# First feed-forward block without Strassen pairs, and the down projection's first inputs in tiles of their own

## Chip, cores and metric

One core of a Trainium2 chip. The metric is the device time of one execution in microseconds (us). Matrix products run on TensorE; VectorE, ScalarE and GpSimd work beside it; SyncE's queue (SP) issues nearly all loads from HBM.

## What is computed

A decoder layer for 256 tokens of width 2048: a mixer with four branches, then a SwiGLU feed-forward part of width 5632, then a last RMSNorm. The change touches the feed-forward part and its two borders:

```python
h = h + mixed @ w_out
v = rms_norm(h, norm_ffn)
h = h + (silu(v @ w_ffn_gate) * (v @ w_ffn_up)) @ w_ffn_down
return rms_norm(h, norm_final)
```

All is float32. Each float32 product is made from three products of a faster format: an operand is split into a high part (ScalarE copies it, rounding) and a low part (VectorE subtracts), and high x high, high x low and low x high are added up in PSUM (`mm3`, `mm3s`).

## The kernel before, in words

**Common way.** The rows of a weight matrix are taken two k-tiles of 128 at a time, here called a k-pair. `wpiece` (lines 117 to 127) loads 256 x 512 weights (512 KB) into a `raw` tile on SP's queue, ScalarE makes `whi`, VectorE makes `wlo`; there are four slots of each. Per piece and block of 128 tokens there are six matmuls of 128 x 512.

**Strassen pairs.** `pair` (lines 243 to 292) multiplies the two token blocks with two column blocks of weights (`wl`, `wr`) at once. A k-pair in `skps` is made by Strassen's scheme with 7 products in place of 8, so 21 matmuls in place of 24. `s_weights` loads both pieces into one `sx` tile (1 MB, two slots), VectorE forms sums (`se`, `sx`) and all are split into `sh`, `sl`, `seh`, `sel`. The activations need four sums too: `s_sums` forms them in a scratch tile and splits them into `vsh`, `vsl`, which have three slots of four 128 x 128 blocks. `pair` adds up in eight PSUM banks named 1 to 8: a Strassen pair writes 1, 5, 7, 6 first and then 2, 3, 4; an ordinary k-pair writes 2, 3, 4, 8. When the last Strassen pair is done, `mid` is called: `mid_sums` combines banks 1, 5, 6, 7 into four tiles `u` (tags `u0` to `u3`). With no Strassen pair, `mid` is called at k-pair 2.

**Gate and up.** Eleven blocks `f` of 512 hidden columns, eight k-pairs each. Blocks 1 to 10 take k-pairs 0, 3 and 5 by Strassen, block 0 takes 0 and 3. After a block, `hd` (two token blocks x 512) is formed from the banks, the `u` tiles, Silu and a scale. `hid_out` is put off (`later`) to the `mid` of the next block: TensorE transposes `hd` (`trans_bank`, two banks), ScalarE copies into a tile `hs`, and GpSimd's queue stores `hs` to DRAM (`hid`, 512 KB) in one transfer.

**Down.** Two halves `cc` of the output columns, 22 k-pairs each, of which 0, 3, 6, 9, 12 go by Strassen. `h_of` loads a k-pair's hidden block from DRAM into `hv` (tags `u1` and `u3` by turns, 256 KB, SP's queue), splits it into one of four slots of `ah` and, for Strassen, forms the sums. `mid` adds the four `u` tiles into `hn`.

**Where things lie.** `sx`, `sh`, `se` and their like are in a pool opened after the mixer's pools are closed, so in the room of the mixer's tiles (`mth` among them). `vth` and `vtl`, the normalised input of gate and up, are in the pool `uv` under tags `th` and `tl`; `gfin` and `ah` of the down part take the same tags.

**Order.** The program is written in Python order; a planner reorders it by a simulated timeline and places all waits. Each engine and each queue then runs in the order given. Only a few instructions are pinned.

Of the kernel before, what the change touches and what calls it, by code (L numbers as in the profile page):

```python
# [8 lines left out]
F32 = mybir.dt.float32  # L9
F32R = mybir.dt.float32r  # L10
AF = mybir.ActivationFunctionType
ALU = mybir.AluOpType
AX = mybir.AxisListType

P = 128
S = 256
D = 2048
NKT = D // P
DFF = 5632
NFT = DFF // P  # L20
# [9 lines left out]
def hybrid_block_kernel(  # L30
# [7 lines left out]
    nc = tc.nc  # L38
# [5 lines left out]
    w_fg = w_ffn_gate[0]  # L44
    w_fu = w_ffn_up[0]
    w_fd = w_ffn_down[0]
# [9 lines left out]
    def act(o, i, f=AF.Copy, **kw):  # L56
        return nc.scalar.activation(o, i, f, **kw)  # L57

    def tt(o, a, b, op, eng=None):
        return (eng or nc.vector).tensor_tensor(out=o, in0=a, in1=b, op=op)  # L60
# [6 lines left out]
    def stt(o, a, s, b, op0, op1, **kw):  # L67
        return nc.vector.scalar_tensor_tensor(out=o, in0=a, scalar=s, in1=b, op0=op0, op1=op1, **kw)

    late = {"psum": None, "turn": 0}  # L70
# [7 lines left out]
    def rd(t):  # L78
        return t.bitcast(F32)
# [116 lines left out]

    def s_sums(v, sh, sl):

        w = late["tmp"].tile([P, 512], F32, tag="u0", name="ssum").rearrange("p (a b) -> p a b", a=4)
        a11, a21, a12, a22 = v[:, 0, 0:P], v[:, 0, P:S], v[:, 1, 0:P], v[:, 1, P:S]
        tt(w[:, 0, :], a21, a22, ALU.subtract)
        tt(w[:, 1, :], w[:, 0, :], a11, ALU.subtract)
        tt(w[:, 2, :], a11, a21, ALU.subtract)
        tt(w[:, 3, :], a12, w[:, 1, :], ALU.add)
        act(sh, w)
        tt(sl, w, rd(sh), ALU.subtract)
# [28 lines left out]
    def pair(wl, wr, nkp, skps, a_of, sx, mid, split=0):  # L237


        pq = late["psum"]  # L240
        names = (1, 5, 7, 6, 2, 3, 4, 8) if skps else (2, 3, 4, 8)
        b = {i: pq.tile([P, 512], F32, tag=f"p{i}", name=f"p{i}") for i in names}
        left = {2: nkp * 2 - len(skps), 3: nkp * 2 - len(skps), 4: nkp * 2 - len(skps), 8: 2 * (nkp - len(skps))}
        for i in (1, 5, 6, 7):
            left[i] = len(skps)
        begun = set()

        def go(i, a, w, pin=False):
            left[i] -= 1
            mm3s(b[i], a, w, i not in begun, left[i] == 0, pin)  # L250
            begun.add(i)

        held = []
        for kp in range(nkp):
            blk, sums = a_of(kp, kp in skps)
            if kp in skps:
                l1, l2, r2, t1, t2, t3, t4 = s_weights(wl, wr, kp, sx)
                go(1, blk(0, 0), l1)
                go(5, sums(0), t1)
                go(7, sums(2), t3)  # L260
                go(6, sums(1), t2)
                go(2, blk(1, 0), l2)
                go(3, sums(3), r2)
                go(4, blk(1, 1), t4)
                if kp == skps[-1]:
                    mid(b)
                continue
            if not skps and kp == 2:
                mid(b)
            rows = slice(kp * 2 * P, (kp + 1) * 2 * P)  # L270
            lh, ll = wpiece(wl[rows, :], 2, 512)
            rh, rl = wpiece(wr[rows, :], 2, 512)
            todo = [(i, [(blk(j, t), (wh[:, j, :], wl_[:, j, :])) for j in range(2)])
                    for i, t, wh, wl_ in ((2, 0, lh, ll), (3, 0, rh, rl), (4, 1, lh, ll), (8, 1, rh, rl))]
            if kp >= nkp - split:
                held.append(todo)
                continue
            for i, prods in todo:
                for a, w in prods:
                    go(i, a, w)  # L280
        for q in range(4):
            for todo in held:
                i, prods = todo[q]
                for a, w in prods:
                    go(i, a, w, pin=True)
        return b
# [503 lines left out]

    def hid_out(hd, f):

        hs = fp.tile([P, 4, S], F32, tag="hs", name="hs")
        for i in (0, 2):
            pt = trans_bank(hd, i, 2)
            act(hs[:, i:i + 2, :].rearrange("p a b -> p (a b)"), pt)
        d = dr.tile([P, 4, S], F32, name=f"hid{f}")
        nc.gpsimd.dma_start(d, hs)
        hid.append(d)

    def v_of(kp, with_sums):
        def blk(j, t):
# [8 lines left out]
    def mid_sums(b):  # L811

        u = [fp.tile([P, 512], F32, tag=f"u{i}", name="u") for i in range(4)]
        act(u[0], b[1])
        tt(u[2], u[0], b[6], ALU.add)
        tt(u[1], u[2], b[7], ALU.add)
        tt(u[2], b[5], u[2], ALU.subtract)
        tt(u[3], b[5], u[1], ALU.subtract)
        return u
# [5 lines left out]
    for f in range(DFF // 512):  # L825
        fs = slice(f * 512, (f + 1) * 512)
        kept = []

        def mid(b):
            kept.extend(mid_sums(b))  # L830
            run_later()

        b = pair(w_fg[:, fs], w_fu[:, fs], NKT // 2, FS[:2] if f == 0 else FS, v_of, sx, mid, split=1)
        hd = fp.tile([P, 2, 512], F32, tag="hd", name="hd")
        for t in range(2):
            tt(hd[:, t, :], kept[t], b[(2, 4)[t]], ALU.add)
            act(hd[:, t, :], hd[:, t, :], AF.Silu, scale=rstd2[:, t:t + 1])
            tt(kept[2 + t], kept[2 + t], b[(3, 8)[t]], ALU.add)
            stt(hd[:, t, :], kept[2 + t], rstd2[:, t:t + 1], hd[:, t, :], ALU.mult, ALU.mult)
        later.append(lambda hd=hd, f=f: hid_out(hd, f))  # L840


    gfin = uv.tile([P, D], F32, tag="th", name="gfin")
    nc.gpsimd.dma_start(gfin, norm_final.partition_broadcast(P))
    ss3 = small.tile([P, 2, 4], F32, name="ss3", bufs=1)
    pre3 = small.tile([P, 2], F32, name="pre3", bufs=1)
    ah = uv.tile([P, 4, 2, 2 * S], F32R, tag="tl", name="ah")
    DS = (0, 3, 6, 9, 12)

    def h_of(kp, with_sums):  # L850
        v = fp.tile([P, 512], F32, tag=("u1", "u3")[kp % 2], name="hv").rearrange("p (a b) -> p a b", a=2)
        nc.sync.dma_start(v, hid[kp // 2][:, kp % 2 * 2:kp % 2 * 2 + 2, :])
        q = kp % 4
        act(ah[:, q, 0, :], v.rearrange("p a b -> p (a b)"))
        tt(ah[:, q, 1, :], v.rearrange("p a b -> p (a b)"), rd(ah[:, q, 0, :]), ALU.subtract)
        if with_sums:
            i = DS.index(kp) % len(FS)
            s_sums(v, hsh[:, i], hsl[:, i])

        def blk(j, t):  # L860
            o = slice(j * S + t * P, j * S + (t + 1) * P)
            return ah[:, q, 0, o], ah[:, q, 1, o]
        return blk, lambda n: (hsh[:, i, n, :], hsl[:, i, n, :])

    hsh, hsl = vsh, vsl
    for cc in range(2):
        cols = [slice((2 * cc + i) * 512, (2 * cc + i + 1) * 512) for i in range(2)]

        def mid(b):
            u = mid_sums(b)  # L870
            for t in range(2):
                for i in range(2):
                    o = hn[:, t, cols[i]]
                    tt(o, o, u[2 * i + t], ALU.add)
            run_later()

        b = pair(w_fd[:, cols[0]], w_fd[:, cols[1]], NFT // 2, DS, h_of, sx, mid, split=2 if cc else 1)
        for t in range(2):
            for i in range(2):
                o = hn[:, t, cols[i]]  # L880
                tt(o, o, b[((2, 3), (4, 8))[t][i]], ALU.add)
                sumsq(ss3[:, t, 2 * cc + i:2 * cc + i + 1], o)
                if cc == 0 or i == 0:
                    tt(o, o, gfin[:, cols[i]], ALU.mult, nc.gpsimd)
            if cc == 0:
                continue
            ms3, r, z, r3, p3 = (small.tile([P, 1], F32, tag=f"r3{i}", name="r3") for i in range(5))
            nc.vector.tensor_reduce(out=p3, in_=ss3[:, t, 0:3], axis=AX.X, op=ALU.add)
            ts(p3, p3, 1.0 / D, EPS, ALU.mult, ALU.add)
            stt(ms3, ss3[:, t, 3:4], 1.0 / D, p3, ALU.mult, ALU.add)  # L890
            tt(r, ms3, mhalf[:, 0:1], ALU.pow, nc.gpsimd)
            tc.keep_in_program_order(tt(o, o, gfin[:, cols[1]], ALU.mult))
            stt(z, ms3, r, r, ALU.mult, ALU.mult)
            ts(z, z, -0.5, 1.5, ALU.mult, ALU.add)
            tt(r3, r, z, ALU.mult)
            for i in range(4):
                o = hn[:, t, i * 512:(i + 1) * 512]
                if i % 2:
                    act(o, o, scale=r3)
                else:  # L900
                    ts(o, o, r, z, ALU.mult, ALU.mult)
                nc.sync.dma_start(out[t * P:(t + 1) * P, i * 512:(i + 1) * 512], o)
# [31 lines left out]
```

## Time and profile before

| | us |
|---|---|
| median of 3 runs | 1555.77 (1554.59 to 1556.63) |
| the profiled execution | 1554.03 |
| its span | 1552.3 |

| engine | busy us | share of the span |
|---|---|---|
| TensorE, matmuls | 1506.3 | 97% |
| TensorE, weight loads | 1243.3 | 80% |
| VectorE | 1088.4 | 70% |
| ScalarE | 794.3 | 51% |
| GpSimd | 102.0 | 7% |

Mean granted TensorE clock of the span: 0.987 of full speed. The gate/up blocks run from 803 to 1279 us of the span, the down part from there to 1542.

How to read the rows: times are microseconds from the start of the span. A matmul's record lasts longer than the distance to the next one, as they are pipelined; a record is about 0.39 us. "[4.87 <-ACT ah L57]" says that the engine was idle for 4.87 us before this instruction, and that the wait was ended by ScalarE's write of `ah` in line 57. Lines 57, 60, 65 and 68 are helpers for one operation of ScalarE or VectorE each; tiles tell them apart. PE is TensorE, ACT ScalarE, DVE VectorE, POOL GpSimd, SPq and POOLq the queues on which DMAs are issued.

### The profile page before, as it was taken

Reading aid. Unit: us, or ns where it says so; the run is one execution under the profiler, and the core shown is the slowest. Engines: PE = TensorE matmul, PEld = TensorE weight load, DVE = VectorE, ACT = ScalarE, POOL = GpSimd, SP = SyncE. Lnnn points to the kernel's source line nnn. Section 1 sums busy time; section 2 is a strip of 40 time slices with the busy share of each in tenths; the row PEclk is TensorE's granted clock in tenths of the full one; section 3 lists DMA queues with packets and bytes.
Section 4 is the critical chain, followed back from the end, with each engine's and each line's share of the span. In section 5 each row is a group of like instructions: output and inputs, shape, how many; then the busy total and the mean of one; then the engine's idle time right before and its main releaser. Section 6 shows DMA issues by size and latency. Waiting matters only on the chain.

```text
span 1552.3 us, 18562 instructions
## 1 busy us (share of the span) xinstructions
PE 1506.3 (97%) x6823; PEld 1243.3 (80%) x6823; DVE 1088.4 (70%) x1324; ACT 794.3 (51%) x940; POOL 102.0 (7%) x108
## 2 busy tenths in 40 slices
PE   8999999999999999999989999999999999889987
PEld 7878888888888888888868888888888877768865
DVE  4756645776565555555669988889888987957854
ACT  5555844544444444444545655555555555635533
POOL 4000300011111021010000000000000000001001
PEclk9999999999999999999999999999999999989999
DMA  7655555566666676767666666666666667766553
GB/s 232 214 149 159 154 174 152 170 183 203 199 202 197 199 208 197 208 191 244 184 209 216 199 222 219 203 215 215 208 204 214 217 218 240 236 207 218 188 177 128
DMA packets 158171, 309.44 MB, mean 199 GB/s; under 512 B 10432, under 2 KB 12544, under 8 KB 157952
## 3 DMA queue, kind: packets, MB, share of 16 engines
q1 hardware_dynamic: 154496, 296.82, 61.7%
q0 software_dynamic: 3552, 11.44, 2.4%
q8 instruction: 53, 0.87, 0.2%
q14 instruction: 38, 0.31, 0.1%
q10 hardware_dynamic: 32, 0.01, 0.0%
HBM read 300.36 MB, written 7.86 MB: 199 GB/s over the span
## 4 chain that ended last, share of the span: by engine, by line
PE 90%; DVE 4%; DMA 3%; issue 2%; ACT 1%; SPq 0%; POOL 0%; POOLq 0%; ACTq 0%; DVEq 0%
PE acc L133 47%; PE p L213 38%; DMA hv<-hid 2%; PE ps L165 2%; DVE wlo L60 1%; DVE sl L60 1%; DVE se L60 1%; DVE u L60 1%; DMA xq<-in_x_dram 0%; DMA sx<-in_w_ffn_gate_dram 0%; DVE hn L60 0%; PE ps L489 0%; PE ps L685 0%; PE ps L508 0%; PE ps L447 0%
## 5 line engine op out<-in xcount | busy, mean ns | idle before, releaser
L60 DVE TENSOR_TENSOR wlo<-raw,whi 128x1024 fp32r<-128x1024 f32 (+1 forms) x452 | 560.9, 1242 | 336.6 <-ACT whi L57 332.7
L57 ACT ACTIVATE whi<-raw 128x1024 fp32r<-128x1024 f32 (+1 forms) x452 | 474.8, 1052 | 526.4 <-PE acc L133 304.5
L133 PE MATMUL acc<-wlo,uth 128*128 128x512 f32 (+1 forms) x832 | 323.7, 390 | 0.0
L133 PE MATMUL acc<-whi,utl 128*128 128x512 f32 (+1 forms) x832 | 323.2, 389 | 0.0
L133 PE MATMUL acc<-whi,uth 128*128 128x512 f32 (+1 forms) x832 | 317.7, 391 | 0.6 <-DVE nat L64 0.4
L213 PE MATMUL p<-whi,ah 128*128 128x512 f32 x544 | 172.2, 396 | 17.6 <-ACT ah L57 17.6
L133 PEld LDWEIGHTS acc<-wlo,uth 128*128 128x128 f32 x832 | 156.9, 189 | 31.7 <-issue 1.0
L133 PEld LDWEIGHTS acc<-whi,utl 128*128 128x128 f32 x832 | 156.9, 189 | 31.4 <-issue 0.7
L133 PEld LDWEIGHTS acc<-whi,uth 128*128 128x128 f32 x832 | 154.2, 189 | 31.9 <-issue 0.7
L213 PE MATMUL p<-whi,vth 128*128 128x512 f32 x448 | 175.2, 391 | 1.0 <-DVE hn L60 1.0
L213 PE MATMUL p<-wlo,vth 128*128 128x512 f32 x448 | 175.1, 391 | 0.0
L213 PE MATMUL p<-whi,vtl 128*128 128x512 f32 x448 | 174.3, 391 | 0.0
L213 PEld LDWEIGHTS p<-whi,ah 128*128 128x128 f32 x544 | 104.2, 191 | 40.1 <-ACT ah L57 18.2
L60 DVE TENSOR_TENSOR sl<-sx,sh 128x2048 fp32r<-128x2048 f32 x42 | 96.1, 2288 | 50.1 <-ACT sh L57 50.1
L57 ACT ACTIVATE sh<-sx 128x2048 fp32r<-128x2048 f32 x42 | 80.5, 1917 | 93.6 <-PE p L213 84.3
L213 PE MATMUL p<-wlo,ah 128*128 128x512 f32 x272 | 107.8, 397 | 0.0
L213 PEld LDWEIGHTS p<-whi,vth 128*128 128x128 f32 x448 | 84.2, 188 | 18.5 <-issue 1.4
L213 PEld LDWEIGHTS p<-whi,vtl 128*128 128x128 f32 x448 | 84.2, 188 | 17.1
L213 PEld LDWEIGHTS p<-wlo,vth 128*128 128x128 f32 x448 | 84.1, 188 | 17.0
L60 DVE TENSOR_TENSOR sel<-se,seh 128x1536 fp32r<-128x1536 f32 x42 | 73.6, 1752 | 1.1 <-ACT seh L57 1.1
L57 ACT ACTIVATE seh<-se 128x1536 fp32r<-128x1536 f32 x42 | 61.9, 1473 | 0.8 <-DVE se L60 0.6
L213 PEld LDWEIGHTS p<-wlo,ah 128*128 128x128 f32 x272 | 52.4, 193 | 11.1
(299 smaller groups left out, 1855.1 us busy)
## 6 DMA issues: line engine op xcount, KB each, us to landing
raw<-in_w_in_dram SPq DMA_DIRECT2D x192, 512.0 KB, 3.6
raw<-in_w_ffn_down_dram SPq DMA_DIRECT2D x68, 512.0 KB, 4.7
raw<-in_w_ffn_gate_dram SPq DMA_DIRECT2D x56, 512.0 KB, 3.8
raw<-in_w_ffn_up_dram SPq DMA_DIRECT2D x56, 512.0 KB, 4.6
raw<-in_w_branch_dram SPq DMA_DIRECT2D x32, 512.0 KB, 4.0
raw<-in_w_out_dram SPq DMA_DIRECT2D x32, 512.0 KB, 3.9
sx<-in_w_ffn_up_dram SPq DMA_DIRECT2D x32, 512.0 KB, 3.8
sx<-in_w_ffn_gate_dram SPq DMA_DIRECT2D x32, 512.0 KB, 4.8
```

Of the source, the lines that this page charges most:

```text
L57: return nc.scalar.activation(o, i, f, **kw)
L60: return (eng or nc.vector).tensor_tensor(out=o, in0=a, in1=b, op=op)
L133: m = nc.tensor.matmul(acc, x_, w_, start=st, stop=sp_)
L165: nc.tensor.transpose(pt[:, i * S + t * P:i * S + (t + 1) * P], nat[:, t, (c0 + i) * P:(c0 + i + 1) * P], ident)
L213: m = nc.tensor.matmul(acc, x_, w_, start=st, stop=sp_)
```

## The change

- Gate/up block 0 has no Strassen pairs. `mid` there forms no `u` tiles; Silu and the product read the banks directly.
- `hid_out` writes the transposed block back into `hd` and stores it from there in two transfers of 256 KB, one for each half, to 22 DRAM tiles of one k-pair each. `hs` is gone.
- The first four hidden blocks are loaded into `ht_first`, a slot of tag `sx`. In the first half, k-pairs 0 and 1 are split into slots of `vsh` and `vsl`.
- Later hidden blocks are loaded into three pieces of `fin`, the tile that also holds `gfin`; the scratch for the sums is a fourth piece. Tags `u1`, `u3` and `u0` are no longer used for them.
- Strassen pairs of the down part are 3, 6, 9, 12, 15.

```diff
-    def s_sums(v, sh, sl):
-
-        w = late["tmp"].tile([P, 512], F32, tag="u0", name="ssum").rearrange("p (a b) -> p a b", a=4)
+    def s_sums(v, sh, sl, w=None):
+
+        if w is None:
+            w = late["tmp"].tile([P, 512], F32, tag="u0", name="ssum")
+        w = w.rearrange("p (a b) -> p a b", a=4)
...
     def hid_out(hd, f):
-        hs = fp.tile([P, 4, S], F32, tag="hs", name="hs")
         for i in (0, 2):
             pt = trans_bank(hd, i, 2)
-            act(hs[:, i:i + 2, :].rearrange("p a b -> p (a b)"), pt)
-        d = dr.tile([P, 4, S], F32, name=f"hid{f}")
-        nc.gpsimd.dma_start(d, hs)
-        hid.append(d)
+            o = hd[:, :, i * P:(i + 2) * P]
+            act(o, pt.rearrange("p (a b) -> p a b", a=2))
+            d = dr.tile([P, 2 * S], F32, name=f"hid{2 * f + i // 2}")
+            nc.gpsimd.dma_start(d.rearrange("p (a b) -> p a b", a=2), o)
+            hid.append(d)
...
         def mid(b):
-            kept.extend(mid_sums(b))
+            if 1 in b:
+                kept.extend(mid_sums(b))
             run_later()
 
-        b = pair(w_fg[:, fs], w_fu[:, fs], NKT // 2, FS[:2] if f == 0 else FS, v_of, sx, mid, split=1)
+        b = pair(w_fg[:, fs], w_fu[:, fs], NKT // 2, () if f == 0 else FS, v_of, sx, mid, split=1)
         hd = fp.tile([P, 2, 512], F32, tag="hd", name="hd")
         for t in range(2):
-            tt(hd[:, t, :], kept[t], b[(2, 4)[t]], ALU.add)
-            act(hd[:, t, :], hd[:, t, :], AF.Silu, scale=rstd2[:, t:t + 1])
-            tt(kept[2 + t], kept[2 + t], b[(3, 8)[t]], ALU.add)
-            stt(hd[:, t, :], kept[2 + t], rstd2[:, t:t + 1], hd[:, t, :], ALU.mult, ALU.mult)
+            g, u = b[(2, 4)[t]], b[(3, 8)[t]]
+            if kept:
+                tt(hd[:, t, :], kept[t], g, ALU.add)
+                tt(kept[2 + t], kept[2 + t], u, ALU.add)
+                g, u = hd[:, t, :], kept[2 + t]
+            act(hd[:, t, :], g, AF.Silu, scale=rstd2[:, t:t + 1])
+            stt(hd[:, t, :], u, rstd2[:, t:t + 1], hd[:, t, :], ALU.mult, ALU.mult)
...
-    gfin = uv.tile([P, D], F32, tag="th", name="gfin")
+    ht_first = sx.tile([P, 4, 512], F32, tag="sx", name="ht_first", bufs=2)
+    for kp in range(4):
+        nc.sync.dma_start(ht_first[:, kp, :], hid[kp])
+    fin = uv.tile([P, 2 * D], F32, tag="th", name="fin")
+    gfin = fin[:, :D]
...
-    DS = (0, 3, 6, 9, 12)
+    DS = (3, 6, 9, 12, 15)
 
-    def h_of(kp, with_sums):
-        v = fp.tile([P, 512], F32, tag=("u1", "u3")[kp % 2], name="hv").rearrange("p (a b) -> p a b", a=2)
-        nc.sync.dma_start(v, hid[kp // 2][:, kp % 2 * 2:kp % 2 * 2 + 2, :])
-        q = kp % 4
-        act(ah[:, q, 0, :], v.rearrange("p a b -> p (a b)"))
-        tt(ah[:, q, 1, :], v.rearrange("p a b -> p (a b)"), rd(ah[:, q, 0, :]), ALU.subtract)
+    def h_of(cc, kp, with_sums):
+        if cc == 0 and kp < 4:
+            v = ht_first[:, kp, :]
+        else:
+            v = fin[:, D + kp % 3 * 512:D + (kp % 3 + 1) * 512]
+            nc.sync.dma_start(v, hid[kp])
+        if cc == 0 and kp < 2:
+            hi, lo = (t[:, kp].rearrange("p a b -> p (a b)") for t in (vsh, vsl))
+        else:
+            hi, lo = ah[:, kp % 4, 0, :], ah[:, kp % 4, 1, :]
+        act(hi, v)
+        tt(lo, v, rd(hi), ALU.subtract)
         if with_sums:
-            i = DS.index(kp) % len(FS)
-            s_sums(v, hsh[:, i], hsl[:, i])
+            i = (DS.index(kp) + 2) % len(FS)
+            s_sums(v.rearrange("p (a b) -> p a b", a=2), vsh[:, i], vsl[:, i], fin[:, D + 1536:])
```

## Rows read from the trace of the kernel before

**Rows 1.** The page: busy us of each engine, share of the span, instructions.
```profile
PE 1506.3 (97%) x6823; PEld 1243.3 (80%) x6823; DVE 1088.4 (70%) x1324; ACT 794.3 (51%) x940; POOL 102.0 (7%) x108
```
**Rows 2.** Who TensorE waited for, whole span: us in total, times, longest.
```profile
PE p L213 <- ACT ah L57: 22.4, 3, 11.4
PE p L213 <- ACT sh L57: 5.6, 1, 5.6
...
PE p L213 <- DVE hn L60: 1.0, 1, 1.0
```
**Rows 3.** Timeline of TensorE: start, us, engine, line, operation, [idle before <-releaser].
```profile
811.58 0.79 PE L213 MATMUL p<-sh,vth 128*128 128x512 f32 x1 [5.62 <-ACT sh L57]
...
1283.80 0.59 PE L213 MATMUL p<-sh,ah 128*128 128x512 f32 x1 [4.87 <-ACT ah L57]
...
1365.30 0.80 PE L213 MATMUL p<-whi,ah 128*128 128x512 f32 x1 [11.43 <-ACT ah L57]
...
1489.92 0.79 PE L213 MATMUL p<-whi,ah 128*128 128x512 f32 x1 [6.13 <-ACT ah L57]
```
**Rows 4.** TensorE by stretch: bounds, length, busy (matmuls), granted clock, DMA share, GB/s.
```profile
811.50:816.50 5.00, 4.92 (x12) 0.51 0.28 73
...
1283.80:1287.60 3.80, 3.80 (x10) 0.55 0.96 331
1365.30:1369.60 4.30, 4.30 (x11) 0.52 0.38 122
1489.90:1497.00 7.10, 7.08 (x19) 0.59 0.46 145
```
**Rows 5.** Timeline of the SP queue: DMAs issued (start, us of issuing).
```profile
711.43 3.53 SPq L769 DMA_DIRECT2D hn<-in_x_dram  x4
...
802.40 0.37 SPq L220 DMA_DIRECT2D sx<-in_w_ffn_up_dram  x1
...
1278.48 0.34 SPq L852 DMA_DIRECT2D hv<-hid  x1
...
1358.98 11.40 SPq L852 DMA_DIRECT2D hv<-hid  x5
```
**Rows 6.** Chain of work that ended last: start, us, what; a stretch of unbroken matmuls.
```profile
889.22 43.58 PE p L213 x192
```
**Rows 7.** Timeline of VectorE: first write of `hd` in block 2.
```profile
936.47 0.68 DVE L60 TENSOR_TENSOR hd<-u,p 128x512 f32<-128x512 f32 x1
```
**Rows 8.** Timeline of GpSimd: stores of `hs` in blocks 2, 3, 10.
```profile
935.77 0.53 POOL L798 DMA_DIRECT2D hid<-hs  x1 [45.02 <-ACT hs L57]
975.03 0.53 POOL L798 DMA_DIRECT2D hid<-hs  x1 [38.73 <-ACT hs L57]
...
1275.28 0.53 POOL L798 DMA_DIRECT2D hid<-hs  x1 [45.08 <-ACT hs L57]
```
**Rows 9.** Timeline of TensorE: thirteenth matmul of blocks 2 and 3.
```profile
899.54 0.39 PE L213 MATMUL p<-sh,vth 128*128 128x512 f32 x1
...
941.97 0.39 PE L213 MATMUL p<-sh,vth 128*128 128x512 f32 x1
```
**Rows 10.** The page: DMA issues, count, KB each, median us to landing.
```profile
hid<-hs POOLq DMA_DIRECT2D x11, 512.0 KB, 5.3
bb<-in_b_gate_dram POOLq DMA_DIRECT2D x16, 256.0 KB, 4.3
```
**Rows 11.** Engines by stretch: busy (instructions) of PE, PEld, DVE, ACT, POOL; clock.
```profile
896.90:939.30 42.40, 42.40 (x193) 35.10 (x192) 37.08 (x39) 23.16 (x22) 0.53 (x1) 1.00 0.66 214
...
1300.00:1350.00 50.00, 50.00 (x222) 41.40 (x221) 48.11 (x61) 31.00 (x32) 0.00 (x0) 1.00 0.78 256
```
**Rows 12.** DMA issues from 974.5 to 975.5 alone: block 3's store.
```profile
hid<-hs POOLq DMA_DIRECT2D x1, 512.0 KB, 6.6
```
**Rows 13.** Timeline of ScalarE: first copy into `hs` in blocks 1 and 2.
```profile
887.69 0.58 ACT L57 ACTIVATE hs<-ps 128x512 f32<-128x512 f32 x1
...
933.27 0.60 ACT L57 ACTIVATE hs<-ps 128x512 f32<-128x512 f32 x1 [0.47 <-PE ps L165]
```

More of the change, by code (lines that the diff above doesn't have):

```diff
@@ L847, in hybrid_block_kernel @@
     ah = uv.tile([P, 4, 2, 2 * S], F32R, tag="tl", name="ah")
-    DS = (0, 3, 6, 9, 12)
-    def h_of(kp, with_sums):
-        v = fp.tile([P, 512], F32, tag=("u1", "u3")[kp % 2], name="hv").rearrange("p (a b) -> p a b", a=2)
-        nc.sync.dma_start(v, hid[kp // 2][:, kp % 2 * 2:kp % 2 * 2 + 2, :])
-        q = kp % 4
-        act(ah[:, q, 0, :], v.rearrange("p a b -> p (a b)"))
-        tt(ah[:, q, 1, :], v.rearrange("p a b -> p (a b)"), rd(ah[:, q, 0, :]), ALU.subtract)
+    DS = (3, 6, 9, 12, 15)
[11 more added lines that the diff above has]
+        tt(lo, v, rd(hi), ALU.subtract)
         if with_sums:
-            i = DS.index(kp) % len(FS)
-            s_sums(v, hsh[:, i], hsl[:, i])
+            i = (DS.index(kp) + 2) % len(FS)
+            s_sums(v.rearrange("p (a b) -> p a b", a=2), vsh[:, i], vsl[:, i], fin[:, D + 1536:])
         def blk(j, t):
             o = slice(j * S + t * P, j * S + (t + 1) * P)
-            return ah[:, q, 0, o], ah[:, q, 1, o]
-        return blk, lambda n: (hsh[:, i, n, :], hsl[:, i, n, :])
-    hsh, hsl = vsh, vsl
+            return hi[:, o], lo[:, o]
+        return blk, lambda n: (vsh[:, i, n, :], vsl[:, i, n, :])
     for cc in range(2):
@@ L875, in mid @@
             run_later()
-        b = pair(w_fd[:, cols[0]], w_fd[:, cols[1]], NFT // 2, DS, h_of, sx, mid, split=2 if cc else 1)
+        b = pair(w_fd[:, cols[0]], w_fd[:, cols[1]], NFT // 2, DS, lambda kp, ws: h_of(cc, kp, ws), sx, mid, split=2 if cc else 1)
         for t in range(2):
```

## Prediction

> **What bounds the kernel now.** I read the page's busy times first, then who TensorE waited for over the whole span, then the timeline around each of those waits. The page gives TensorE 97% of the span, VectorE 70% [rows 1]: TensorE sets the time, and only its idle stretches and its slow stretches can be won back without removing products. The waits in the feed-forward part are few [rows 2]: three for ScalarE's `ah` (22.4 us together), one for ScalarE's `sh` (5.6 us), one of 1.0 us for `hn`. They sum to 29.0 us; none lies in gate/up blocks 1 to 10. The timeline places the four large ones [rows 3]: 5.62 us in front of 811.58 (first gate/up block), 4.87 in front of 1283.80 (gate/up to down), 11.43 in front of 1365.30 and 6.13 in front of 1489.92 (both just behind the down projection's `mid`). Sum 28.05 us.
>
> Behind each of them the matmuls run at the lower clock level. The granted clock is 0.51, 0.55, 0.52 and 0.59 (near 1.2 GHz of 2.4) in the 5.0, 3.8, 4.3 and 7.1 us that follow [rows 4]. Stretch times (1 - clock) is what is lost: 2.45 + 1.71 + 2.06 + 2.91 = 9.13 us. The four sites therefore cost 28.05 + 9.13 = 37.2 us. That is all that this change can reach.
>
> **Why they wait.** First block: its first Strassen pair (k-pair 0) needs `sx`, whose pool lies where the mixer's tiles were; its load goes out only at 802.40 [rows 5], when the last matmul on `mth` is through, while ordinary `raw` pieces, which have a pool of their own, are loaded long before. Change to down: `hv` of k-pair 0 lives in tag `u1`, of k-pair 1 in `u3`, tiles that the last gate/up block still reads when it forms `hd`; so the load goes out at 1278.48 [rows 5], and lands and is split before the first product can start. Behind `mid`: the same tags are the `u` of `mid_sums`; `mid`'s additions into `hn` free them only after TensorE has run out, and five `hv` loads follow in a row from 1358.98 [rows 5].
>
> **The change, part by part.** *First block in the common way.* It has no Strassen pairs, so it never looks at `sx`. The 5.62 and 2.45 us go. Two pairs of 21 products become 24: six matmuls more at 43.58 us / 192 = 0.227 us [rows 6] is 1.36 us, straight on the path. VectorE and ScalarE lose two weight sums and one `mid_sums`; neither is on the path there, so I count nothing. The sums for block 1 are then formed beside block 0's products; `sx` can be loaded from 802.40, some 43 us before it is used. The 1.0 us wait for `hn` is a bank released by the last `w_out` chunk; other banks are now touched first, so it may stay or go: 0 to -1.0, I take 0. Net -6.7 us.
>
> *Inputs ahead.* `ht_first` is a slot of tag `sx`, freed two Strassen pairs back, so its four loads (hidden blocks 0 and 1, long stored) run in the last gate/up block. K-pairs 0 and 1 are split into `vsh`/`vsl` slots 0 and 1, last read by the last block's k-pairs 0 and 3. The first products of down then need no load issued after the change of stage. K-pairs 2 and 3 go to `ah`, free once the last gate/up matmul is done; they are needed two ordinary k-pairs (48 matmuls, 10.9 us) later. That covers two splits on ScalarE and VectorE. If that cover were gone, the price is at most the old 4.87 + 1.71. The slot costs a later load for down's k-pair 6, which is used some 32 us into the stage: nothing.
>
> *Later k-pairs.* `hv` now turns over three pieces of `fin`, and the sums' scratch another piece; no tag is shared with `mid_sums`. So the 11.43 + 2.06 and 6.13 + 2.91 us go. What is late next there is VectorE: `mid` puts eight additions of 0.68 us on it, 5.5 us, but it now lies behind k-pair 15, with only ordinary k-pairs left and two of those already split ahead (four `whi`/`wlo` slots are 10.9 us of products). I take 0 and price the miss below. The count of Strassen pairs in down stays five per half.
>
> *The wait that is added.* `hid_out` transposes in place: `hd` itself is the source of two stores instead of `hs` of one. A new `hd` must wait until both have landed; before, it waited for the transposes only. Behind the first addition into `hd` on VectorE stand the other three evacuations, the next `wlo` and `sx` sums; ScalarE's Silu and then TensorE's next use of bank 2 wait for it. Even-numbered blocks are tight: the old store is issued at 935.77, `hd` is written at 936.47 and bank 2 is needed by the matmul at 941.97 [rows 7 to 9] (the thirteenth of the next block; twelve come first on other banks). The trace has no 256 KB store from GpSimd; the same queue's 512 KB store takes 5.3 us and its 256 KB load 4.3 us [rows 10], which is nearer in size, so I take 4.3. Then `hd` is free at 940.1 and the bank, one 0.68 us addition later, at 940.8: 1.2 us to spare. VectorE stands up to 3.6 us, but has 42.4 - 37.1 = 5.3 us idle in such a block [rows 11]. Odd blocks: issued 975.03 [rows 8], 6.6 us for the 512 KB [rows 12], so landed 981.6 even so and the bank free at 982.3; due one block of 42.4 us after 941.97, at 984.4. So 0 for blocks 1 to 9; with 5.3 us still 0.2 us to spare.
>
> At the change to down it is not free. K-pair 0 is now ordinary and starts on banks 2, 3, 4, 8, without the 12 products on other banks that shield them elsewhere. Store issued 1275.28 [rows 8], landed 1279.6, addition done 1280.3, due at 1278.8, when the last gate/up product is through: a new wait of 1.4 us (0 if the store lands in 2.8 us, 2.4 us if in 5.3; with the slow clock of the old wait here, 1.7 us more).
>
> The page DMA: Bandwidth & Descriptors of the Trainium skill (Anatomy of one DMA) prices a GpSimd DMA at about 2.0 us plus bytes over 436 GB/s; an estimate from it is 2.6 us for 256 KB, and by it the new wait would be gone. For 512 KB the page gives 3.2 us where the trace has 5.3 [rows 10], so the trace does not agree and the sum goes by the rows.
>
> The page Perfetto Trace Analysis of the Trainium skill (DMA Optimizations) speaks against the split: transfers under 2 KB carry significant overhead, and the new stores read 1 KB pieces of `hd`. No row here shows that for a store; by it the landing would stay nearer 5.3 than 4.3, and the sum would lose 1 us.
>
> **Sum.** 37.2 won, 1.36 paid for products, 1.4 for the new wait: 34.4 us. The profiled execution took 1554.03 us (span 1552.3 and 1.7 around it); 1554.03 - 34.4 = 1519.6. It lies 1.7 us under the median of 1555.77, so the median comes to 1521.4.
>
> **Rivals.** *Halves in series, short* (chance 0.12). The two column halves of `hd` interleave in memory. If they count as overlapping, the second copy waits for the first store: copy, store L, copy, store L. The first copy starts at 933.27 in an even block, 2.5 us ahead of the store's issue [rows 8, 13]; with 0.6 us a copy, 0.3 to the issue and the addition's 0.7, bank 2 is free at 935.8 + 2L against 942.0 in four even blocks, and at 1275.3 + 2L against 1278.8 at the change. With L = 4.3: 4 x 2.4 + 5.1 + 1.7 (clock) = 16.4 us, 15 more than in my sum: 1536. For it: the trace before has no such pair of reads and writes. Against: the four `hn` loads, column slices of one tile in the same pattern, are issued within 3.5 us [rows 5] and don't wait for one another.
>
> *Halves in series, long: the slower side* (0.04). The same place, and odd blocks join: first copy at 887.69, bank due at 899.54 [rows 9, 13], free at 890.2 + 2L. Total 4(2L - 6.2) + 5(2L - 9.3) + (2L - 3.5) + 1.7 = 20L - 73, against 37.2 - 1.36 = 35.8 won: it decides from L = 5.4 us on, just above the median store today. With L = 6.6, as an odd block's store takes [rows 12], 59 us are lost: 1555.8 - 35.8 + 59 = 1579. Against it: it needs the overlap and no gain from halving the store.
>
> *VectorE becomes the bound in down* (0.12). It is 48.1 of 50 us busy in the Strassen stretch [rows 11]. K-pairs 3 to 15 are 5 x 21 + 8 x 24 = 297 products, 67.4 us; at that rate VectorE needs 64.8 for them, and `mid`'s 5.5 make 70.3: short by 2.9 us a half if three ordinary k-pairs ahead give it no lead, by 8.4 if `mid` also comes when nothing is split ahead: 6 to 17 us, 1527 to 1538. Against it: TensorE did not wait once in that stretch, though VectorE entered it late.
>
> *It doesn't do what it says* (0.06): the planner puts the `ht_first` loads or the splits so that the change of stage waits as long as before, 4.87 + 1.71 where I count 1.4: 5.2 us more, 1527.
>
> **How the numbers follow.** My forecast 0.66, bounds 1517 (no new wait, the 1.0 us gone, and the 2 us by which the runs of before differ) to 1526 (the new wait 2.4 with slow clock, 2 us between runs). Rivals 0.12, 0.12, 0.06, 0.04. The range 1516 to 1538 takes in all but the slower rival, with a little over for what I have not named. Faster by over 0.2% (3.1 us, about what a measurement of this kernel can tell from no change): all but the slower rival and 0.02 between: 0.94. Same 0.02, slower 0.04.
>
> **What would show it.** Right: no wait for `sh` near 806; matmuls on `whi` follow the last `w_out` product within 1 us; first wait at the change of stage 0 to 2.5 us, ended by VectorE's `hd` (or the Silu) and not by `ah`; no stretch under 0.9 clock after it; no idle behind either `mid`; TensorE's products up by six. Wrong: VectorE idle before `hd` ended by a store, TensorE waiting for bank 2 in every second block; or TensorE waiting for `sel`, `wlo` or `ah` between k-pairs 6 and 17.

## The result, and the profile after

| | before | after |
|---|---|---|
| median of 4 runs, us | 1555.74 (1554.59 to 1556.63) | 1522.04 (1519.15 to 1522.67) |
| ratio | | 0.978 (95% interval 0.9763 to 0.9797) |
| the profiled execution, its span | 1554.03, 1552.3 | 1522.67, 1521.0 |
| first product of gate and up, in the span | 802.98 | 806.10 |
| from there to the end | 749.3 | 714.9 |

The forecast was 1521.4 us, in a range of 1516 to 1538. The last line of the table is the part that the change touches: span less start of the first product on `vth`. It fell by 34.4 us, which is the sum of the prediction; that it agrees to the tenth is luck, as a second profile of after gives 35.4 (below). In the profiled run after, the mixer ahead of it, whose code is the same, took 3.1 us longer; that is told of at the end.

Who TensorE waited for after, whole span (us in total, times, longest), beside [rows 2]:

```profile
PE ps L165 <- DMA xq<-in_x_dram: 3.6, 1, 3.6
PE ps L165 <- ACT dqn L57: 1.5, 1, 1.5
...
PE p L215 <- DVE u L60: 1.1, 2, 0.7
PE p L215 <- DVE hn L60: 1.0, 1, 1.0
```

The waits for `ah` (22.4 us) and `sh` (5.6 us) are gone; `hn` stayed at 1.0 and 1.1 us for `u` came in. Line 215 of after is line 213 of before. The waits on line 165 for `xq` and `dqn` are in the mixer. The page of after, beside [rows 1]:

```profile
PE 1501.8 (99%) x6829; PEld 1240.0 (82%) x6829; DVE 1075.2 (71%) x1308; ACT 790.7 (52%) x939; POOL 110.5 (7%) x119
```

TensorE has six matmuls more, as said, and 11 GpSimd instructions more, the second stores. The four old sites by stretch after (bounds, length, busy and count of PE, PEld, DVE, ACT, POOL, then granted clock, DMA share, GB/s), beside [rows 4]:

```profile
800.00:825.00 25.00, 24.02 (x110) 19.68 (x109) 19.06 (x25) 14.53 (x19) 0.71 (x1) 1.00 0.81 273
1275.00:1300.00 25.00, 23.87 (x103) 19.02 (x103) 21.23 (x33) 14.71 (x19) 0.56 (x1) 1.00 0.94 335
1350.00:1375.00 25.00, 25.00 (x116) 20.68 (x115) 24.71 (x29) 14.65 (x17) 1.36 (x2) 1.00 0.79 252
1475.00:1500.00 25.00, 25.00 (x112) 20.69 (x111) 15.52 (x19) 9.73 (x12) 0.00 (x0) 1.00 0.49 161
```

The clock is 1.00 in all four; TensorE is full but for 1.0 us (`hn`) at the start and 1.1 at the change to down. The bill by rows: idle time 29.0 before less 2.1 after is 26.9, the slow stretches 9.1, less 1.4 for the six products: 34.6, against 34.4 measured.

### The profile page after: what moved, and what is told of

Its sections match the earlier page's. It is cut to its first block, busy times and chain, and to the rows that moved or that the text cites. A ratio compares the mean times of both kernels' runs of the same rounds, so it can differ in the third digit from the quotient of the medians.

```text
span 1521.0 us, 18622 instructions
## 1 busy us (share of the span) xinstructions
PE 1501.8 (99%) x6829; PEld 1240.0 (82%) x6829; DVE 1075.2 (71%) x1308; ACT 790.7 (52%) x939; POOL 110.5 (7%) x119
## 4 chain that ended last, share of the span: by engine, by line
PE 95%; DVE 2%; DMA 1%; issue 1%; ACT 1%; POOL 0%; SPq 0%; POOLq 0%; ACTq 0%; DVEq 0%
PE acc L133 47%; PE p L215 44%; PE ps L165 2%; DMA sx<-in_w_ffn_down_dram 1%; DMA xq<-in_x_dram 0%; DMA raw<-in_w_in_dram 0%; DVE wlo L60 0%; PE ps L491 0%; PE ps L687 0%; PE ps L510 0%; PE ps L449 0%; DVE sl L60 0%; PE ps L557 0%; DVE u L60 0%; ACT whi L57 0%
## 5 line engine op out<-in xcount | busy, mean ns | idle before, releaser
L215 PE MATMUL p<-whi,vtl 128*128 128x512 f32 x464 | 181.2, 391 | 0.0
L215 PE MATMUL p<-wlo,vth 128*128 128x512 f32 x464 | 180.9, 391 | 0.0
L215 PE MATMUL p<-whi,vth 128*128 128x512 f32 x464 | 179.5, 391 | 1.0 <-DVE hn L60 1.0
L215 PE MATMUL p<-whi,ah 128*128 128x512 f32 x512 | 160.1, 389 | 0.0
L215 PEld LDWEIGHTS p<-whi,ah 128*128 128x128 f32 x512 | 96.1, 188 | 19.9
L60 DVE TENSOR_TENSOR sl<-sx,sh 128x2048 fp32r<-128x2048 f32 x40 | 91.5, 2288 | 27.4 <-ACT sh L57 27.3
L215 PE MATMUL p<-wlo,ah 128*128 128x512 f32 x256 | 99.7, 390 | 0.0
L60 DVE TENSOR_TENSOR se<-sx 128x512 f32<-128x512 f32 x80 | 54.9, 686 | 3.5 <-DMA sx<-in_w_ffn_down_dram 2.3
```

The lines of the kernel that those rows point to most:

```text
L215: m = nc.tensor.matmul(acc, x_, w_, start=st, stop=sp_)
```

## The experiments

For every kernel the profile gives the same measure: span less start of the first product on `vth`, here "feed-forward part". Two profiles of after give 714.9 and 713.9; 714.4 is taken for it, and "above after" below means a feed-forward part longer than that; differences of about 1 us say nothing. Ratios are against the kernel before, run on the same chip with them.

| kernel | median us | ratio, 95% interval | feed-forward part |
|---|---|---|---|
| before | 1555.74 | | 749.3 |
| after | 1522.04 | 0.978 (0.9763 to 0.9797) | 714.9 |
| after again | 1520.22 | 0.9775 (0.9758 to 0.9792) | 713.9 |
| before + first block | 1547.95 | 0.9941 (0.992 to 0.9963) | 744.2 |
| after - first block | 1527.94 | 0.9817 (0.9796 to 0.9837) | 722.2 |
| after - `ht_first` | 1528.71 | 0.9822 (0.9801 to 0.9844) | 722.2 |
| after, old tags | 1535.13 | 0.9852 (0.9823 to 0.988) | 727.2 |
| after, old tags swapped | 1541.08 | 0.9911 (0.9894 to 0.9927) | 735.8 |
| after, `hs` back | 1518.52 | 0.9778 (0.9757 to 0.9799) | 713.3 |
| the same again | 1518.93 | 0.9766 (0.9747 to 0.9785) | 714.1 |
| after, stores twice | 1520.28 | 0.9781 (0.9764 to 0.9797) | 715.9 |
| after, two Strassen pairs in block 0 | 1529.38 | 0.9839 (0.9824 to 0.9854) | 723.6 |

### The first block alone, and all but the first block

Of the diff only the edits to `mid`, to `pair`'s list and to the forming of `hd` go into the kernel before:

```diff
-        b = pair(..., FS[:2] if f == 0 else FS, v_of, sx, mid, split=1)
+        b = pair(..., () if f == 0 else FS, v_of, sx, mid, split=1)
```

> The kernel before with the first gate/up block formed in the common way and nothing else. Theory (each site was priced by its own idle and slow stretch): the 5.62 us wait and the 2.45 us of slow clock go, six products come (1.36 us), so 6.7 us less: about 1549.0 us, and the waits at the change to down and behind both mids stay at 4.9, 11.4 and 6.1 us. Rival (the first block's wait only moves, since block 1's sums now wait for the same loads): no wait near 806 but one of 3 us or more in front of the second block, total within 2 us of 1555.7. The part before the first gate/up product holds the same code as the kernel before (802.98 us there) and is expected within 1 us of it.

The feed-forward part is 5.1 us shorter than before, where the theory had 6.7; by the medians on the same chip it is 7.2 us (1555.15 to 1547.95). TensorE's waits in it:

```profile
PE p L213 <- ACT ah L57: 23.2, 3, 11.6
...
PE p L213 <- DVE hn L60: 1.0, 1, 1.0
```

No `sh`, and no new wait in the block. The three waits for `ah` are 0.8 us more than in [rows 2], which is half of the 1.6 us that are missing. The other half lies behind the first of them, where the slow stretch is worse (the 7.5 us from the end of the wait at the change to down, the kernel before and then this one: bounds, length, busy and count of matmuls, granted clock, DMA share, GB/s):

```profile
1283.80:1291.30 7.50, 7.50 (x26) 0.77 0.62 216
1276.80:1284.30 7.50, 7.50 (x22) 0.63 0.59 223
```

That is 7.5 x 0.14, about 1.0 us. So what is missing was lost at the down part's old waits and not in the first block, as far as one profile of each can tell. The rival, that the wait only moves to another place, falls.

The other half, on the kernel after:

```diff
-        b = pair(..., () if f == 0 else FS, v_of, sx, mid, split=1)
+        b = pair(..., FS[:2] if f == 0 else FS, v_of, sx, mid, split=1)
```

> The changed kernel with the two Strassen pairs of the first block put back; all that concerns the down projection stays. Theory: the waits at the change to down and behind both mids stay gone, the first block waits its 5.6 us again and runs 2.45 us slow, six products fewer: 6.7 us more than the changed kernel, about 1528.7 us. Rival (the parts share a cause, the sx slots): the wait in the first block is also shorter or the change to down waits more than 3 us again; total off 1528.7 by over 3 us.

7.8 us above after, by the medians 5.9 to 7.7, where the theory had 6.7; the rival falls. The one large wait is that of [rows 3], back in its place, with slow matmuls behind it:

```profile
813.19 0.79 PE L215 MATMUL p<-sh,vth 128*128 128x512 f32 x1 [5.94 <-ACT sh L57]
...
800.00:825.00 25.00, 18.08 (x69) 14.16 (x68) 18.72 (x24) 11.46 (x12) 0.72 (x1) 0.86 0.62 210
```

So the two halves of the change add up to within 2.7 us: 5.1 + 27.1 (749.3 - 722.2) is 32.2, against 34.9 for both; some 1.8 us of that are the longer waits and slower matmuls just told of, the rest stays open.

### Down without `ht_first`

```diff
-    ht_first = sx.tile([P, 4, 512], F32, tag="sx", name="ht_first", bufs=2)
-    for kp in range(4):
-        nc.sync.dma_start(ht_first[:, kp, :], hid[kp])
...
-        if cc == 0 and kp < 4:
-            v = ht_first[:, kp, :]
-        else:
-            v = fin[:, D + kp % 3 * 512:D + (kp % 3 + 1) * 512]
-            nc.sync.dma_start(v, hid[kp])
+        v = fin[:, D + kp % 3 * 512:D + (kp % 3 + 1) * 512]
+        nc.sync.dma_start(v, hid[kp])
```

> The changed kernel without ht_first: all hidden blocks go through the three pieces of fin, which are free only when the last gate/up product is through; k-pairs 0 and 1 still go to vsh and vsl. Theory (the load issued after the change is the wait there): first product of down waits for one 256 KB load (4.2 us) and a split on ScalarE and VectorE (1.3 us), 5.5 us in place of 1.1, plus 1.7 us of slow clock: about 6 us more than the changed kernel, 1528 us. Rival (VectorE's backlog of evacuations sets the change of stage, and the load hides beside it): within 2 us of 1522.

7.8 us above after, by the medians 6.7 to 8.5, where the theory had about 6: the wait was put at 5.5 us and is 6.65. The load of the first hidden blocks goes out at the change of stage again (SP's queue), and TensorE waits for its split:

```profile
1273.29 1.29 SPq L859 DMA_DIRECT2D fin<-hid  x3
...
1280.13 0.80 PE L215 MATMUL p<-whi,vsh 128*128 128x512 f32 x1 [6.65 <-ACT vsh L57]
```

In the kernel after, the loads of `ht_first` go out 50 us ahead:

```profile
1225.37 2.05 SPq L851 DMA_DIRECT2D ht_first<-hid  x4
```

A place of its own for the later loads (`fin`) is not enough here, since `fin` is free only when the last product on `vth` is done; it is the slot of `sx`, free earlier, that carries the change of stage.

### The old tags behind `mid`, and the two swapped

`hv` goes back to the tags of `mid`'s tiles, the sums' scratch to `u0`; all else is as after:

```diff
-            v = fin[:, D + kp % 3 * 512:D + (kp % 3 + 1) * 512]
+            v = fp.tile([P, 512], F32, tag=("u1", "u3")[kp % 2], name="hv")
...
-            s_sums(..., vsh[:, i], vsl[:, i], fin[:, D + 1536:])
+            s_sums(..., vsh[:, i], vsl[:, i])
```

> The changed kernel, but the hidden blocks after the first four go to tags u1 and u3 by turns and the sums' scratch to u0, as before. ht_first, the place of mid (behind k-pair 15) and all else stay. Theory (the shared tags are the cause of the waits behind mid): both waits come back, 13.5 and 9.0 us with their slow clock, now behind k-pair 15: 1522.0 + 22.5 = about 1544 us. Rival (it was the place of mid, with fewer Strassen pairs waiting behind it): no wait behind mid over 1 us, total within 3 us of 1522.

12.8 us above after (by the medians 13.1 to 14.9): the sign and the place are those of the theory, the size is little over half of it. The waits stand behind both `mid`s, but at 4.40 and 4.87 us where [rows 3] have 11.43 and 6.13:

```profile
1366.59 0.79 PE L215 MATMUL p<-whi,ah 128*128 128x512 f32 x1 [4.40 <-ACT ah L57]
...
1490.33 0.79 PE L215 MATMUL p<-whi,ah 128*128 128x512 f32 x1 [4.87 <-ACT ah L57]
```

What differs from the kernel before is where `mid` stands: behind k-pair 15, so that the next k-pair, 16, is even and loads into `u1`; before it stood behind 12, and 13 loads into `u3`. The next kernel swaps the two tags and nothing else:

```diff
-            v = fp.tile([P, 512], F32, tag=("u1", "u3")[kp % 2], name="hv")
+            v = fp.tile([P, 512], F32, tag=("u3", "u1")[kp % 2], name="hv")
```

> The kernel after with hv in the tags of mid's tiles, as in e3_old_tags, but even k-pairs in u3 and odd ones in u1. Theory: the shared tag is what TensorE waits for behind mid, and the wait is the longer the later mid frees the tag that the next k-pair wants; k-pair 16 then loads into u3, which the additions into hn free last, as k-pair 13 did in the kernel before. The waits for ah behind the two mids grow from 4.4 and 4.9 us toward the 11.4 and 6.1 of the kernel before, with the slow clock behind them: 3 to 8 us above e3_old_tags, 1538 to 1543 us. Rival: the order of the two tags is nothing, the waits of e3_old_tags are smaller because mid lies behind k-pair 15: 1533 to 1537 us, waits of 4 to 5 us each.

```profile
1370.38 0.79 PE L215 MATMUL p<-whi,ah 128*128 128x512 f32 x1 [12.15 <-ACT ah L57]
...
1494.32 0.80 PE L215 MATMUL p<-whi,ah 128*128 128x512 f32 x1 [6.08 <-ACT ah L57]
```

21.4 us above after (by the medians 19.0 to 20.9), 1.1 short of the 22.5 of the kernel before, whose waits are back within 0.8 us each. Its median of 1541.08 lies in the theory's range. Why one tag costs so much more than the other is seen on VectorE and SP's queue. Old tags, then swapped:

```profile
1362.49 1.28 DVE L60 TENSOR_TENSOR hn<-hn,u 128x512 f32<-128x512 f32 x2
1363.20 0.34 SPq L865 DMA_DIRECT2D hv<-hid  x1
1365.90 0.63 ACT L57 ACTIVATE ah<-hv 128x512 fp32r<-128x512 f32 x1 [0.98 <-DMA hv<-hid]
```

```profile
1359.74 2.29 DVE L60 TENSOR_TENSOR sl<-sx,sh 128x2048 fp32r<-128x2048 f32 x1
1361.94 0.69 DVE L60 TENSOR_TENSOR hn<-hn,u 128x512 f32<-128x512 f32 x1
1362.05 0.37 SPq L222 DMA_DIRECT2D sx<-in_w_ffn_down_dram  x1
1362.76 0.37 SPq L223 DMA_DIRECT2D sx<-in_w_ffn_down_dram  x1
1363.25 8.80 SPq L865 DMA_DIRECT2D hv<-hid  x4
1369.70 1.28 ACT L57 ACTIVATE ah<-hv 128x512 fp32r<-128x512 f32 x2 [7.23 <-DMA hv<-hid]
```

With `u1` the load goes out as soon as the first of the two additions at 1362.49 is done and lands in 2.7 us. With `u3` it goes out only after the last addition, which the planner put behind a `sl` of 2.29 us; it then stands behind two loads of 512 KB on the same queue, and takes 6.4 us to land (the DMA issues of that moment alone, `u1` with the old tags, `u3` with them swapped: count, KB, us to landing):

```profile
hv<-hid SPq DMA_DIRECT2D x1, 256.0 KB, 2.7
```

```profile
hv<-hid SPq DMA_DIRECT2D x1, 256.0 KB, 6.4
```

Two kernels that differ only in the order of two tags are 8.7 us apart in the feed-forward part, and 6.0 by their medians.

### What the stores from `hd` cost

The transposed halves go into `hs` again and are stored from there, still in two:

```diff
+        hs = fp.tile([P, 4, S], F32, tag="hs", name="hs")
...
-            o = hd[:, :, i * P:(i + 2) * P]
+            o = hs[:, i:i + 2, :]
```

> The changed kernel, but the transposed half blocks are copied into a tile hs again and stored from there (two stores as in the changed kernel), so that a new hd waits for the transposes alone. If the wait for the stores costs TensorE what the prediction took (1.4 us at the change to down, measured 1.1 there): 1.1 us less, about 1520.9 us, and no wait of TensorE between 1274 and 1280. Rival (the 1.1 us come from VectorE's own backlog in front of the evacuation of banks 3 and 8, and the planner has put other work into the wait for the stores): the 1.1 us stay, total within 0.5 us of 1522.0, VectorE's 7.8 us of waits for stores gone all the same.

In after, the wait at the change to down is this (TensorE, then VectorE):

```profile
1275.53 0.47 PE L215 MATMUL p<-whi,vsh 128*128 128x512 f32 x1 [0.35 <-DVE u L60]
...
1278.91 0.50 PE L215 MATMUL p<-whi,vsh 128*128 128x512 f32 x1 [0.75 <-DVE u L60]
1278.17 0.68 DVE L60 TENSOR_TENSOR u<-u,p 128x512 f32<-128x512 f32 x1
1279.57 1.28 DVE L60 TENSOR_TENSOR hd<-u,p 128x512 f32<-128x512 f32 x2
```

With `hs` back it is gone: TensorE runs through the change of stage without a gap in both profiles of that kernel, while both profiles of after have one (1.1 and 0.8 us, the second in part for `ah`). So the stores out of `hd` are behind this wait. But nothing waits for a store there. The later store goes out at 1271.28 and takes 6.1 us, so it has landed by 1277.4, and `hd` is written at 1279.57; the only idle time of VectorE at the change is for weights of the down part (GpSimd, the issue of that moment alone, VectorE):

```profile
1271.28 0.69 POOL L800 DMA_DIRECT2D hid<-hd  x1 [0.74 <-ACT hd L57]
hid<-hd POOLq DMA_DIRECT2D x1, 256.0 KB, 6.1
1274.09 0.69 DVE L60 TENSOR_TENSOR se<-sx 128x512 f32<-128x512 f32 x1 [1.41 <-DMA sx<-in_w_ffn_down_dram]
```

The planner has put both additions into `hd` last, and sums and splits of weights in front of the additions into `u`, so that banks 3 and 8, not bank 2, come late; with `hs` the additions into `hd` and into `u` take turns, `hd` first. What TensorE waits for is this order of VectorE's work, as the rival had it. That the wait goes when the stores leave `hd`, as the theory had it, is then the planner's doing too. This is read from the traces; the order was not changed by itself.

The kernel was run again beside after:

> The kernel of e5_hs_back once more, beside the kernel after on the same chip: transposed halves go to hs and are stored from there in two halves. Theory: without the wait at the change to down it is 1 to 4 us shorter than the kernel after: 1518 to 1521 us. Rival: the wait of 1.1 us is lost in the scatter of the mixer's start: within 1 us of the kernel after.

> The kernel after, unchanged, for the comparison with e9_hs_back_again. Theory: 1521 to 1523 us, 1 to 4 above e9_hs_back_again; from one profile to the other the feed-forward part stays at 715 us within 0.5 while the start of it moves between 801 and 808 us with the waits for xq and dqn. Rival: the feed-forward part itself moves by 2 us or more.

1518.93 against 1520.22, with intervals that overlap; the feed-forward parts are 714.1 and 713.9. The theory of 1 to 4 us rests on medians whose scatter is as large, and the profiles don't carry it: whether `hs` is worth its room stays open, at no more than a microsecond or so. After's own feed-forward part differs by 1.0 us between its two profiles, a little over the 0.5 that was expected.

Each half stored a second time, to a tile that nobody reads:

```diff
             nc.gpsimd.dma_start(d.rearrange("p (a b) -> p a b", a=2), o)
+            nc.gpsimd.dma_start(d2.rearrange("p (a b) -> p a b", a=2), o)
```

> The changed kernel, but each half of hd is stored twice, the second time to a DRAM tile that nothing reads: GpSimd issues four DMAs a block in place of two, and hd is free only when all have landed. Nothing of the result changes. Theory (1.2 us to spare in even blocks, 2 to 3 us more until the last store lands): bank 2 is free 1 to 2 us late in four even blocks, odd blocks keep their spare time, the change to down waits 2 to 3 us more: 6 to 11 us more than the changed kernel, 1528 to 1533 us. Rival (VectorE's idle time and the planner's order take it up): under 2 us more, 1522 to 1524 us.

1.5 us above after in the feed-forward part, nothing by the median: the rival is right. At the change to down TensorE waits 0.9 us in all (0.5 for `ah`, 0.4 for `u`), no longer than in after, where the theory had 2 to 3 us more: once more the landing of the stores is not what it waits for. VectorE stood about as long for the stores with two as with one (after, then stores twice):

```profile
DVE hd L60 <- DMA hid<-hd: 7.8, 5, 1.9
```

```profile
DVE hd L60 <- DMA hidx<-hd: 6.5, 6, 1.8
```

The reading "1.2 us to spare in even blocks" took the order of VectorE in the kernel before [rows 7] for given. In after, `hd` comes behind both `u`:

```profile
936.64 0.68 DVE L60 TENSOR_TENSOR u<-u,p 128x512 f32<-128x512 f32 x1
937.24 0.69 DVE L60 TENSOR_TENSOR se<-se,sx 128x512 f32<-128x512 f32 x1
937.84 1.28 DVE L60 TENSOR_TENSOR hd<-u,p 128x512 f32<-128x512 f32 x2
```

### Two Strassen pairs in block 0 after all

If `sx` is late only for k-pair 0, block 0 could keep k-pairs 3 and 5 and save six products:

```diff
-        b = pair(..., () if f == 0 else FS, v_of, sx, mid, split=1)
+        b = pair(..., FS[1:] if f == 0 else FS, v_of, sx, mid, split=1)
```

> The changed kernel, but the first gate/up block takes k-pairs 3 and 5 by Strassen (k-pair 0 stays ordinary). Theory (only k-pair 0 comes too early for the sx load; k-pair 3 is used 16 us later, and the load and the sums take 9 + 7 us): no wait in the first block, six products fewer than the changed kernel, 1.4 us less: 1520.7 us. Rival (16 us are not enough for both, or the two loads at once hold back the raw pieces): a wait of 1 to 4 us in front of k-pair 3 or 4, total 1522 to 1526 us.

9.2 us above after: both expectations miss. Four waits end between 837 and 845, the first for VectorE's `sl`; in that stretch VectorE is full and TensorE isn't:

```profile
837.34 0.50 PE L215 MATMUL p<-sl,vth 128*128 128x512 f32 x1 [1.96 <-DVE sl L60]
839.61 0.50 PE L215 MATMUL p<-sel,vsh 128*128 128x512 f32 x1 [1.11 <-DVE sel L60]
842.01 1.12 PE L165 MATMUL ps<-ident,hn 128*128 128x128 f32 x4 [0.93 <-DVE u L60]
844.60 0.80 PE L215 MATMUL p<-sh,vth 128*128 128x512 f32 x1 [1.47 <-ACT sh L57]
...
825.00:850.00 25.00, 19.53 (x71) 14.23 (x70) 24.59 (x27) 13.50 (x13) 0.00 (x0) 0.81 0.59 196
```

After has 20.22 us of VectorE in the same stretch and TensorE full:

```profile
825.00:850.00 25.00, 25.00 (x112) 20.69 (x111) 20.22 (x22) 14.21 (x13) 0.00 (x0) 1.00 0.77 246
```

Three Strassen pairs' sums and splits (k-pairs 3 and 5, and block 1's first) fall together once `sx` is there; the six products saved (1.4 us) don't pay for it. That they fall together is how I read the stretch; it was not tried by moving one of them. The waits sum to 5.5 us; the clock of 0.81 costs 3.7 us over the 19.5 us in which TensorE is busy and 4.8 over all 25; 1.4 is saved: 7.8 to 8.9 of the 9.2.

## Why the prediction was right, step by step

- **What bounds it.** Right: the four sites were worth what their idle time and their slow stretches said, 36.0 us won (26.9 + 9.1, the new wait already taken off) against the 37.2 named as the most. By the medians 33.7 us were won here, and 34.7 when after was run again beside before.
- **First block, -6.7.** Right in mechanism; by itself it measured 5.1, as the last step 7.8: the estimate lies between, and the 1.6 us short of it were lost at later waits, by the rows above. The loads of `sx` do go out at the change of stage and harm nobody, and `hn` kept its 1.0 us, as taken.
- **Change to down.** The old wait went for the reason given: without `ht_first` it is back. The new wait was put at 1.4 and measured 1.1 (0.8 in the second profile). That the size fits is luck, for the path was wrong in two places. The store took 6.1 us to land there, not 4.3; by the prediction's own working (issue 1271.28, one addition of 0.7, the last gate/up product through near 1275.2) bank 2 would have been 2.9 us late. And the planner, which that working left out, let TensorE begin on bank 3 and put `hd` last, so that TensorE waited for `u` and no engine for a store. The clock did not fall behind it (1.00 from 1275 to 1300), so the forecast without the extra 1.7 us was the right one of the two.
- **Behind `mid`.** Right: 0 us there after, and the old tags in the worse order bring back 21.4 of the 22.5 (by the medians 19.0 to 20.9). That the tag alone sets the price was too simple: 12.8 or 21.4 us, by which of the two the next k-pair uses.
- **Blocks 1 to 9.** Right at 0, but not by the working given. A store from `hd` of 256 KB took 4.6 us in the median (22 of them; 4.3 was taken from a load of that size). In the even blocks, which were called tight, VectorE waits for no store: in block 2 it writes `hd` at 937.84, 5.8 us behind the issue of the second store (932.03, below), where the kernel before has 0.7 [rows 7, 8]. All its five waits, 1.9 us at the longest, stand in the odd blocks, which were given the room; TensorE waits in none. Twice the stores cost 1.5 us, little more than the 1.0 by which two profiles of one kernel differ.
- **Halves in series** (0.12 and 0.04). Did not happen: the two stores of a block go out 1.6 us apart, where a store takes 2.5 us to land at the least and 4.6 in the median, so the second copy doesn't wait for the first store.

```profile
930.43 0.69 POOL L800 DMA_DIRECT2D hid<-hd  x1 [43.31 <-ACT hd L57]
932.03 0.69 POOL L800 DMA_DIRECT2D hid<-hd  x1 [0.91 <-ACT hd L57]
...
hid<-hd POOLq DMA_DIRECT2D x22, 256.0 KB, 4.6
```

- **VectorE becomes the bound in down** (0.12). Did not happen: in the stretch of [rows 11] it is 44.33 of 50 us busy, less than before, and where it is nearly full behind `mid` (24.71 of 25, shown above) TensorE is full too. In block 0 with two Strassen pairs both were seen together, a full VectorE and a TensorE that waits for it. What was not weighed: the place where the Strassen work of two blocks meets may matter more than the mean. The stretch in after:

```profile
1300.00:1350.00 50.00, 50.00 (x223) 41.40 (x222) 44.33 (x56) 30.84 (x33) 0.00 (x0) 1.00 0.72 241
```

- **It doesn't do what it says** (0.06). Did not happen.
- **The split into 1 KB pieces.** The kernel with `hs` back stores the same 256 KB in pieces of 2 KB, and its median to landing is 4.2 us in both of its profiles, against 4.6 in both of after:

```profile
hid<-hs POOLq DMA_DIRECT2D x22, 256.0 KB, 4.2
```

The Trainium skill, Perfetto Trace Analysis (DMA Optimizations), has small transfers carry overhead; the trace agrees, at 0.4 us a store. In the median the landing is nearer to 4.3 than to 5.3. The 1 us that the sum would have lost by a longer landing was not lost, though the last store took 6.1, since no engine waited for it.

- **The profiled execution.** 1519.6 was forecast and 1522.67 came; the 3.1 us lie ahead of the changed code.

## What to carry to other kernels

Where a stall stands at a change of stage, ask first which tile the late load writes and who had that room before: here the load into such a slot went out late at all four places, and at each the wait came back, if not always at its old size, when that part of the change was left out or undone. (That the room of the mixer's tiles is what holds up the first block's `sx` is read from when its load goes out; it was not tried by itself.) When an instruction gets a new wait, don't take the order of its neighbours from the old trace if a planner sets it; bound the wait, and expect work to be put in front of it. When two tiles take a tag by turns, see which of them the first user after the change of stage gets, and what stands ahead of its load on the queue.

## What was not expected of the hardware

The start of the feed-forward part moved from 801.53 to 807.64 us between the kernels' profiles, though the mixer ahead of it is the same work in all. Part of it is TensorE's wait for a load of `xq` (2.0 to 4.9 us), part a wait for `dqn` near 50 us and what follows it. After, in its two profiles: the matmul behind the wait, and the four microseconds that start one microsecond later:

```profile
50.53 0.91 PE L165 MATMUL ps<-ident,dqn 128*128 128x128 f32 x4 [1.54 <-ACT dqn L57]
51.53:55.53 4.00, 3.88 (x11) 3.06 (x12) 3.97 (x21) 1.99 (x7) 0.00 (x0) 0.63 0.83 251
```

```profile
49.39 0.91 PE L165 MATMUL ps<-ident,dqn 128*128 128x128 f32 x4 [0.51 <-ACT dqn L57]
50.39:54.39 4.00, 3.89 (x17) 3.24 (x18) 3.96 (x21) 1.99 (x7) 0.00 (x0) 1.00 0.87 262
```

It is one program, with 11 matmuls in place of 17. Of the twelve profiles two show the clock fall there, those with waits of 1.54 and 2.07 us (0.63 and 0.58 of full speed, so mostly the level of 1.2 GHz); the ten others waited 0.36 to 1.36 us and kept 1.00. By these two profiles, as an estimate, a microsecond more of idle time so becomes 1.0 + 4 x 0.37 = 2.5 us in the whole, of the size of the scatter between runs of one kernel here. No run varied this wait alone, so that it is what brings the clock down is not shown.
